# Grouped-query attention on one core: ten output staging buffers, K copies on the GpSimd queue, and a re-costed plan with groups of five

## The chip, the core and the metric

The kernel runs on one core of a Trainium2 chip. The metric is the device time of one execution in microseconds (us). Below it is the median of 13 executions; one further view comes from an execution that was profiled, whose own time is given beside its span (first to last instruction).

## What is computed

Eight batches, eight query heads, two K/V heads (each serves four query heads), 1024 positions, head dimension 64, all in float32:

```python
scores = scale * np.matmul(q_group, k_group.transpose(0, 1, 3, 2))
attn = np.exp(scores - scores_max)
attn = attn / (np.sum(attn, axis=-1, keepdims=True) + 1e-08)
output[:, q_start:q_end, :, :] = np.matmul(attn, v_group)
```

## The kernel before, in words

**Tiling.** A job is one batch, one query head and one half of its queries (the even or the odd positions, 512 of them): 8 x 8 x 2 = 128 jobs, in order. A job has eight cells, one for each 128 keys: 1024 cells. For each cell TensorE makes a score tile of 128 keys by 512 queries with one matmul (L351), an engine turns it into exponentials in bf16, and four output matmuls (L414) multiply it with V, to which a column of ones is added so that the sum of the exponentials comes out as column 65. The scores are small, so the maximum is not subtracted.

**Two ways to the exponential.** "A" cells go to ScalarE in pairs: two scores in one PSUM tile (two such tiles), one activation over 128x1024 (`exps`, L362) into a `pa` tile (26 of them). "D" cells go to VectorE: `exp_bits` (L371) turns one score from one of two PSUM banks into the bits of a bf16 in a slot of a `pd` group of four cells, and when a group is full `exp_curve` corrects it in a chain of four operations over the whole group (L386, L392, L402, L406).

**End of a job.** `normalise` takes the reciprocal of the sums (L427), multiplies the output bank with it into a staging tile `ost` (L429, four buffers, and four of `rec`), and stores that from SyncE's queue (L435). There are two output banks, and L429 is what frees one.

**Loading.** `cast` (L248, GpSimd's queue) copies a head of Q, K or V as bf16 to a scratch in DRAM; it waits for the latest score matmul in program order, so that the loads keep pace. `transpose` (L260, SyncE's queue) brings Q and K from there transposed into `qT` and `kT`, in two pieces each. `place_k` (L268, SyncE's queue) copies `kT` in four DMAs into `kset`, a form in which K stands in one half of the partitions and zeros in the other, so that one matmul with 128 rows takes only the wanted half of `qT`. `place_v` (L282, SyncE's queue) brings V in two DMAs. The very first heads are loaded by `first_loads`: K, Q and V of batch 0 in float32, cast on VectorE, ScalarE and GpSimd, and K and Q transposed on TensorE.

**What sets the order.** `make_plan` is a small planner in Python that runs while the program is built. It holds a cost for each operation and, step by step, takes the one that could start first: a score for ScalarE or VectorE, an output matmul group, a normalisation, a step of a chain. Limits keep it in bounds: `LIVE_A` and `LIVE_D` are the tiles in use, `PENDING` the cells on their way through VectorE, and the last `ONLY_A` cells go to ScalarE alone. Its times fix only the order in which instructions are written out; every engine and every queue then runs its own in that order. The loads are sorted in by their lead before a head's first score `th`: the cast of Q at th − 28, of K at th − 38 and V at th − 33, transposes of K from th − 27 and of Q from th − 17, `place_k` at th − 20, `place_v` at th − 15.

Of the kernel before, what the change touches and what calls it, by code (L numbers as in the profile page):

```python
# [11 lines left out]

CURVE_A, CURVE_B = 0.32988085, -0.33401025

GROUP = 4


def make_plan(nj, nkc):
# [3 lines left out]

    QK, PV, EXP, P1, NORM = 0.214, 0.143, 0.925, 0.605, 0.57
    CHAIN = (0.73, 0.73, 1.26, 1.26)
    FROM_PE, FROM_ACT, FROM_DVE = 0.28, 0.18, 0.12
    LIVE_A, LIVE_D, PENDING, ONLY_A = 26, 6, 8, 14
    INF = 1e9
    n = nj * nkc  # L30
    ops = []
# [14 lines left out]
    while normed < nj:  # L46
        best = None
        if nxt < n:
            ta = td = INF
            if open_a is not None:  # L50
                ta = max(pe, open_a["t"])
            elif live["A"] < LIVE_A:
                ta = max(pe, min(a_free))
            if pending < PENDING and nxt < n - ONLY_A and (cur or live["D"] < LIVE_D):
                td = max(pe, min(bank))
            t, to_d = (ta, 0) if ta <= td else (td, 1)
            if t < INF:
                best = min(best or (INF,), (t, 1 + to_d, "qk", to_d))
        for i, s in enumerate(open_jobs):
            for c in rem[s]:  # L60
                at = max(pe, ready.get(s * nkc + c, INF))
                if at < INF:
                    best = min(best or (INF,), (at, 3 + i, "pv", (s, c)))
        if len(open_jobs) < 2 and next_job < nj:
            at = max(pe, min(obank_free), min(ready.get(next_job * nkc + c, INF) for c in range(nkc)))
            if at < INF:
                best = min(best or (INF,), (at, 3 + len(open_jobs), "open", next_job))
        for q, p, kind in ((normq, 0, "norm"), (p1q, 1, "p1"), (chainq, 2, "chain")):
# [1 line left out]
                best = min(best or (INF,), (max(dve, q[0][0]), p, kind, 0))  # L70
        if cur and nxt >= n - ONLY_A and not p1q:
            best = min(best or (INF,), (dve, 9, "flush", 0))
        t, _, kind, arg = best
        if kind == "qk":
            cell = nxt
            nxt += 1
            pe = t + QK
            if not arg:
                if open_a is None:
                    slot = first_free(a_free)  # L80
                    a_id += 1
                    live["A"] += 1
                    open_a = {"slot": slot, "t": a_free[slot], "cells": []}
                    a_free[slot] = INF
                o = open_a
                ops.append((t, "qk", cell, "A", a_id, o["slot"], len(o["cells"])))
                o["cells"].append(cell)
                home[cell] = ("A", a_id)
                if len(o["cells"]) == 2 or nxt >= n:
                    act = max(act, pe + FROM_PE)  # L90
                    ops.append((act, "exp", a_id, tuple(o["cells"])))
                    act += EXP * len(o["cells"]) / 2
                    a_free[o["slot"]] = act + FROM_ACT
                    uses[("A", a_id)] = len(o["cells"])
                    for x in o["cells"]:
                        ready[x] = act + FROM_ACT
                    open_a = None
            else:
                k = first_free(bank)
                bank[k] = INF  # L100
                pending += 1
                ops.append((t, "qk", cell, "D", k, 0, 0))
                p1q.append((pe + FROM_PE, cell, k))
        elif kind == "open":
            o = first_free(obank_free)
            obank[arg] = o
            obank_free[o] = INF
            open_jobs.append(arg)
            rem[arg] = list(range(nkc))
            next_job += 1  # L110
        elif kind == "pv":
            s, c = arg
            cell = s * nkc + c
            opens = len(rem[s]) == nkc
            rem[s].remove(c)
            done = not rem[s]
            ops.append((t, "pv", s, cell, opens, done, obank[s]))
            pe = t + PV
            h = home[cell]
            uses[h] -= 1  # L120
            if not uses[h]:
                live[h[0]] -= 1
            if done:
                open_jobs.remove(s)
                normq.append((pe + FROM_PE, s))
        elif kind == "norm":
            s = normq.pop(0)[1]
            ops.append((t, "norm", s))
            dve = t + NORM
            obank_free[obank[s]] = dve + FROM_DVE  # L130
            normed += 1
        elif kind == "p1":
            _, cell, k = p1q.pop(0)
            if not cur:
                d_id += 1
                live["D"] += 1
            ops.append((t, "p1", cell, k, d_id, len(cur)))
            dve = t + P1
            bank[k] = dve + FROM_DVE
            cur.append(cell)  # L140
            home[cell] = ("D", d_id)
            if len(cur) == GROUP:
                chainq.append((dve, d_id, cur, 0))
                cur = []
        elif kind == "flush":
            chainq.append((dve, d_id, cur, 0))
            cur = []
        else:
            _, g, cells, step = chainq.pop(0)
            ops.append((t, "chain", g, len(cells), step))  # L150
            dve = t + CHAIN[step] * len(cells) / GROUP
            if step + 1 < len(CHAIN):
                chainq.insert(0, (dve, g, cells, step + 1))
            else:
                pending -= len(cells)
                uses[("D", g)] = len(cells)
                for x in cells:
                    ready[x] = dve + FROM_DVE
# [4 lines left out]
def kernel(  # L163
# [25 lines left out]
    NQS = QBS // 128  # L189
    E1 = D + 1  # L190
    PIECE = 256
    scale = 1.0 / math.sqrt(D)
    bits_scale = 128.0 * scale * math.log2(math.e)
    bits_bias = 128.0 * 127.0
# [12 lines left out]
    first_pool = ctx.enter_context(tc.tile_pool(name="firstp", bufs=1))  # L207
    qT_pool = ctx.enter_context(tc.tile_pool(name="qTpool", bufs=8))
    kT_pool = ctx.enter_context(tc.tile_pool(name="kTpool", bufs=4))
    pa_pool = ctx.enter_context(tc.tile_pool(name="papool", bufs=26))  # L210
    pd_pool = ctx.enter_context(tc.tile_pool(name="pdpool", bufs=6))
    tmp_pool = ctx.enter_context(tc.tile_pool(name="tmppool", bufs=2))
    ostage_pool = ctx.enter_context(tc.tile_pool(name="ostage", bufs=4))
    recip_pool = ctx.enter_context(tc.tile_pool(name="recip", bufs=4))

    def psum_pools(name, n):
        return [
# [21 lines left out]
    qT = {}  # L239
# [25 lines left out]
        transpose(("k", b, g), kT[(b, g)], n)  # L265

    def place_k(b, g, side, parity):
        nc.sync.dma_start(  # L268
            out=ksets[b % 2][
                side * D : (side + 1) * D, g, side, parity * HALF : (parity + 1) * HALF  # L270
            ],
# [16 lines left out]

    def first_loads():

        staged = []
        for eng, src in ((nc.sync, k[0, 0]), (nc.scalar, q[0, 0])):
            f = first_pool.tile([128, NHC, 2, D], FP32, name=f"f{len(staged)}")
            eng.dma_start(
                out=f, in_=src.rearrange("(c p two) d -> p c two d", p=128, two=2)
            )
            staged.append(f)
        vf = first_pool.tile([128, NHC, 2, D], FP32, name="vf")
        nc.sync.dma_start(
            out=vf, in_=v[0, 0].rearrange("(c p two) d -> p c two d", p=128, two=2)  # L300
        )
        cast(("q", 0, 1), q[0, 1])
        for two in range(2):
            nc.gpsimd.tensor_copy(
                out=vsets[0][:, 0, two * NHC : (two + 1) * NHC, 0:D],
                in_=vf[:, :, two, :],
            )
        for side in range(2):
            nc.gpsimd.memset(ksets[1][(1 - side) * D : (2 - side) * D, :, side, :], 0.0)  # L309
        fk, fq = staged  # L310

        hk = first_pool.tile([128, NHC, 3, D], BF16, name="hk")
        nc.vector.tensor_copy(out=hk[:, :, 0:2, :], in_=fk)  # L313
        nc.vector.tensor_copy(out=hk[:, :, 2, :], in_=fk[:, :, 0, :])
        hq = first_pool.tile([128, NHC, 2 * D], BF16, name="hq")
        nc.scalar.copy(out=hq, in_=fq.rearrange("p c two d -> p c (two d)"))
        tk = dbanks[0].tile([128, 2, HALF], BF16, name="dps0")
        tq = dbanks[1].tile([128, HALF], BF16, name="dps1")
        for w in range(2):
            for c in range(NHC):  # L320
                nc.tensor.transpose(  # L321
                    tk[:, w, c * 128 : (c + 1) * 128],
                    hk[:, c, w : w + 2, :].rearrange("p w d -> p (w d)"),
                    ident,
                )
        for c in range(NHC):
            nc.tensor.transpose(tq[:, c * 128 : (c + 1) * 128], hq[:, c, :], ident)
        qT[(0, 0)] = qT_pool.tile([128, HALF], BF16, name="qT")
        lo, hi = slice(0, D), slice(D, 2 * D)
        nc.vector.tensor_copy(out=ksets[0][lo, 0, 0, 0:HALF], in_=tk[lo, 0, :])  # L330
        nc.scalar.copy(out=qT[(0, 0)], in_=tq)
        nc.vector.tensor_copy(out=ksets[0][lo, 0, 0, HALF:S], in_=tk[lo, 1, :])
        nc.vector.tensor_copy(out=ksets[0][hi, 0, 1, 0:HALF], in_=tk[hi, 1, :])
        nc.vector.tensor_copy(out=ksets[0][hi, 0, 1, HALF:S], in_=tk[hi, 0, :])

    p_of = {}
    psum = {}
# [168 lines left out]
```

## Time and profile before

| | |
|---|---|
| median of 13 executions | 443.45 us (441.13 to 448.04) |
| profiled execution | 442.64 us, span 440.9 us |
| busy: TensorE, VectorE, ScalarE, GpSimd | 375.9, 375.8, 385.8, 55.1 us |
| mean granted clock of TensorE | 0.973 |
| exponentials on ScalarE, cells on VectorE | 412 (two cells each), 200 |
| DMA: transposes, stores, K copies, V copies, casts | 156, 128, 60, 30, 93 |

How to read the lines: PE is TensorE, PEld its weight loads, DVE VectorE, ACT ScalarE, POOL GpSimd, SP SyncE; SPq and POOLq are their DMA issues. L351 is line 351 of the kernel. "Idle before, <-" names what ended an engine's idle time just ahead of an instruction. In a line of waits stand the total in us, the number of times and the longest. In a timeline stand start, length, engine, line, operation, tiles, and how many were merged. In a table by stretch stands the busy time of each engine, then the granted clock (1.00 is full), the DMA share and GB/s. In a group the last figures are busy us, mean ns of one, and idle us before them. In a tile's view durations are minimum/median/maximum in ns.

### The profile page before, as it was taken

What the parts mean: (1) busy time and instruction counts of PE and PEld (TensorE: products, weight loads), DVE (VectorE), ACT (ScalarE), POOL (GpSimd) and SP (SyncE); (2) the same over time, 40 slices, a digit from 0 to 9 for tenths busy, and PEclk for the clock granted to TensorE, in tenths of its full rate; (3) what the DMA queues carried; (4) which work ended last, traced back from release to release, by engine and by line L of the source; (5) the groups of instructions that cost most, each with busy time, mean ns of one, the idle gap of its engine ahead of it and who ended that gap; (6) DMA issues with size and microseconds to landing.
All of it is one profiled execution on the core that took longest, in us unless ns stands there. A gap on an engine that the chain in (4) does not pass through costs nothing.

```text
span 440.9 us, 12680 instructions
## 1 busy us (share of the span) xinstructions
PE 375.9 (85%) x5043; PEld 235.7 (53%) x5132; DVE 375.8 (85%) x664; ACT 385.8 (88%) x415; POOL 55.1 (13%) x105
## 2 busy tenths in 40 slices
PE   4788799599996999789979969998959998797995
PEld 2355465355654556455655545565536655454654
DVE  5898798599996998789898959979959998698995
ACT  4899699499996999879989977998959999799993
POOL 5311101001010110101111110110101101100000
PEclk9999899789998999989999998999989999999999
DMA  3854566547576484656647565574755747555314
GB/s 95 132 97 91 116 114 112 111 90 115 108 123 116 89 134 84 121 105 110 115 95 138 111 109 97 103 130 99 121 105 91 126 91 125 110 100 113 74 38 85
DMA packets 137771, 46.73 MB, mean 106 GB/s; under 512 B 130848, under 2 KB 136224, under 8 KB 136224
## 3 DMA queue, kind: packets, MB, share of 16 engines
q1 hardware_dynamic: 134208, 33.46, 36.2%
q0 software_dynamic: 2976, 12.20, 21.3%
q8 instruction: 40, 0.66, 0.7%
q10 hardware_dynamic: 528, 0.26, 0.2%
q14 instruction: 19, 0.16, 0.1%
HBM read 27.13 MB, written 28.97 MB: 127 GB/s over the span
## 4 chain that ended last, share of the span: by engine, by line
DVE 42%; PE 19%; DMA 13%; ACT 13%; SPq 6%; issue 5%; POOL 1%; DVEq 0%; ACTq 0%
ACT pa L362 13%; DMA out_dram<-ost 10%; DVE pd L371 10%; PE aps L351 9%; DVE y L402 8%; DVE pd L406 8%; PE ops L414 8%; DVE ost L429 6%; DVE y L392 4%; SPq L260 4%; DVE z L386 3%; DVE rec L427 2%; PE dps L351 2%; DMA qT<-scr_q 1%; SPq L282 1%
## 5 line engine op out<-in xcount | busy, mean ns | idle before, releaser
L362 ACT ACTIVATE pa<-aps 128x1024 bf16<-128x1024 f32 x412 | 383.3, 1050 | 42.6 <-PE aps L351 30.1
L351 PE MATMUL aps<-qT,kset 128*128 128x512 bf16 x735 | 232.0, 388 | 14.9 <-ACT pa L362 11.5
L414 PEld LDWEIGHTS <-pa 128*128 128x128 bf16 x3296 | 138.1, 99 | 91.5 <-issue 20.3
L414 PE MATMUL ops<-vset,pa 128*128 128x65 bf16 x3296 | 149.8, 195 | 32.3 <-DVE ost L429 28.4
L371 DVE TENSOR_SCALAR pd<-dps 128x512 uint16<-128x512 f32 x200 | 129.8, 682 | 2.2 <-PE dps L351 2.1
L351 PEld LDWEIGHTS <-kset 128*128 128x128 bf16 x1024 | 84.9, 99 | 66.5 <-issue 32.0
L429 DVE TENSOR_TENSOR ost<-ops,rec 128x256 f32<-128x256 f32 x128 | 54.4, 425 | 47.4 <-DMA out_dram<-ost 43.6
L248 POOL DMA_DIRECT2D scr_q<-in_q_dram x63 | 34.7, 552 | 300.3 <-PE aps L351 259.1
L351 PE MATMUL dps<-qT,kset 128*128 128x512 bf16 x200 | 66.0, 387 | 0.9
L406 DVE TENSOR_TENSOR pd<-pd,y 128x2048 uint16<-128x2048 uint16 x50 | 61.2, 1225 | 1.7
L402 DVE TENSOR_TENSOR y<-z,y 128x2048 f16<-128x2048 uint16 x50 | 61.2, 1225 | 1.7
L414 PEld LDWEIGHTS <-pd 128*128 128x128 bf16 x800 | 38.2, 97 | 38.0 <-DVE pd L406 17.4
L414 PE MATMUL ops<-vset,pd 128*128 128x65 bf16 x800 | 45.3, 194 | 7.8 <-DVE pd L406 6.4
L392 DVE TENSOR_SCALAR y<-z 128x2048 f16<-128x2048 uint16 x50 | 34.3, 687 | 0.6
L386 DVE TENSOR_SCALAR z<-pd 128x2048 uint16<-128x2048 uint16 x50 | 34.2, 684 | 0.0
L427 DVE RECIPROCAL rec<-ops 128x4 f32<-128x4 f32 x128 | 22.4, 175 | 4.4 <-PE ops L414 3.8
L248 POOL DMA_DIRECT2D scr_k<-in_k_dram x15 | 7.7, 513 | 22.4 <-PE aps L351 16.9
L248 POOL DMA_DIRECT2D scr_v<-in_v_dram x15 | 7.5, 502 | 15.5 <-PE aps L351 14.7
L321 PE MATMUL dps<-ident,hk 128*128 128x128 bf16 x8 | 1.0, 310 | 5.1 <-DVE hk L313 5.1
L309 POOL MEMSET kset<- 64x2048 bf16 x2 | 3.6, 1798 | 0.1
L321 PEld LDWEIGHTS <-hk 128*128 128x128 bf16 x8 | 0.8, 140 | 5.1 <-DVE hk L313 5.1
L236 DVE MEMSET kset<- 64x1024 uint32 x2 | 1.8, 912 | 1.3 <-PEq L490 1.0
(19 smaller groups left out, 7.9 us busy)
## 6 DMA issues: line engine op xcount, KB each, us to landing
out_dram<-ost SPq DMA_DIRECT2D x128, 128.0 KB, 2.7
scr_q<-in_q_dram POOLq DMA_DIRECT2D x63, 128.0 KB, 3.1
kset<-kT SPq DMA_DIRECT2D x60, 64.0 KB, 2.9
qT<-scr_q SPq DMA_TRANSPOSE x126, 3.2
scr_k<-in_k_dram POOLq DMA_DIRECT2D x15, 128.0 KB, 3.3
scr_v<-in_v_dram POOLq DMA_DIRECT2D x15, 128.0 KB, 3.5
vset<-scr_v SPq DMA_DIRECT2D x30, 64.0 KB, 3.0
kT<-scr_k SPq DMA_TRANSPOSE x30, 3.5
```

Source lines behind the costliest of these rows:

```text
L248: dma = nc.gpsimd.dma_start(out=scr.rearrange("(p f) -> p f", f=1024), in_=src.rearrange("(p s) d -> p (s d)", s=1024 // D),)
L260: nc.sync.dma_start_transpose(out=dst[:, rows], in_=src[rows, :])
L351: last_score[0] = nc.tensor.matmul(dst, lhsT=ksets[b % 2][:, h // HPG, side, c * 128 : (c + 1) * 128], rhs=qT[(b, h)], start=True, stop=Tr ...
L362: nc.scalar.activation(out=pt[:, 0:m], in_=psum.pop(("A", n))[:, 0:m], func=AF.Exp, scale=scale)
L371: nc.vector.tensor_scalar(out=groups[g][:, slot], in0=psum.pop(cell), scalar1=bits_scale, scalar2=bits_bias, op0=ALU.mult, op1=ALU.add,)
L386: nc.vector.tensor_scalar(out=z, in0=pd, scalar1=0x7F, scalar2=None, op0=ALU.bitwise_and)
L392: nc.vector.tensor_scalar(out=y, in0=temps[g][0], scalar1=CURVE_A / 128.0, scalar2=CURVE_B, op0=ALU.mult, op1=ALU.add,)
L402: nc.vector.tensor_tensor(out=y, in0=z, in1=y, op=ALU.mult)
L406: nc.vector.tensor_tensor(out=pd, in0=pd, in1=y, op=ALU.add)
L414: nc.tensor.matmul(ops_of[s][:, qs, :], lhsT=p_of[cell][:, qs * 128 : (qs + 1) * 128], rhs=vsets[b % 2][:, h // HPG, c, :], start=opens an ...
L427: nc.vector.reciprocal(out=rec, in_=o[:, :, D])
L429: nc.vector.tensor_tensor(out=ost, in0=o[:, :, 0:D], in1=rec.unsqueeze(2).to_broadcast([128, NQS, D]), op=ALU.mult,)
```

## The change

Ten `ost` and ten `rec` buffers in place of four. `place_k` issues from GpSimd's queue. Groups of five cells in place of four, with 32 `pa` and five `pd` tiles. The plan has new costs, each with a fixed part and one by the cell for the exponential and the chain; a score for ScalarE may be put `AHEAD` (0.08) earlier in the order than its bank is free; no output matmuls before 2.0; the last 26 cells go to ScalarE alone. `first_loads` brings K and Q in halves, moves the cast of Q head 1 behind GpSimd's copies of V, runs 28 matmuls on the identity ahead of the first transposes, and takes the transposes and copies half by half.

```diff
-GROUP = 4
+GROUP = 5
...
-    QK, PV, EXP, P1, NORM = 0.214, 0.143, 0.925, 0.605, 0.57
-    CHAIN = (0.73, 0.73, 1.26, 1.26)
+    QK, PV, P1, NORM = 0.216, 0.122, 0.605, 0.57
+    EXP, CHAIN = (0.067, 0.4267), ((0.20, 0.133),) * 2 + ((0.19, 0.27),) * 2
     FROM_PE, FROM_ACT, FROM_DVE = 0.28, 0.18, 0.12
-    LIVE_A, LIVE_D, PENDING, ONLY_A = 26, 6, 8, 14
+    LIVE_A, LIVE_D, PENDING, ONLY_A, AHEAD, FIRST_PV = 32, 5, 7, 26, 0.08, 2.0
...
-                best = min(best or (INF,), (t, 1 + to_d, "qk", to_d))
+                early = 0.0 if to_d else AHEAD
+                best = min(best or (INF,), (t - early, 1 + to_d, "qk", to_d, t))
...
-                at = max(pe, ready.get(s * nkc + c, INF))
+                at = max(pe, FIRST_PV, ready.get(s * nkc + c, INF))
...
-            at = max(pe, min(obank_free), min(ready.get(next_job * nkc + c, INF) for c in range(nkc)))
+            at = max(pe, FIRST_PV, min(obank_free), min(ready.get(next_job * nkc + c, INF) for c in range(nkc)))
...
-        t, _, kind, arg = best
+        t, _, kind, arg = best[:4]
         if kind == "qk":
+            t = best[4]
...
-                    act += EXP * len(o["cells"]) / 2
+                    act += EXP[0] + EXP[1] * len(o["cells"])
...
-            dve = t + CHAIN[step] * len(cells) / GROUP
+            dve = t + CHAIN[step][0] + CHAIN[step][1] * len(cells)
...
+    WARM = 28
...
-    pa_pool = ctx.enter_context(tc.tile_pool(name="papool", bufs=26))
-    pd_pool = ctx.enter_context(tc.tile_pool(name="pdpool", bufs=6))
+    pa_pool = ctx.enter_context(tc.tile_pool(name="papool", bufs=32))
+    pd_pool = ctx.enter_context(tc.tile_pool(name="pdpool", bufs=5))
...
-    ostage_pool = ctx.enter_context(tc.tile_pool(name="ostage", bufs=4))
-    recip_pool = ctx.enter_context(tc.tile_pool(name="recip", bufs=4))
+    ostage_pool = ctx.enter_context(tc.tile_pool(name="ostage", bufs=10))
+    recip_pool = ctx.enter_context(tc.tile_pool(name="recip", bufs=10))
...
     def place_k(b, g, side, parity):
-        nc.sync.dma_start(
+        nc.gpsimd.dma_start(
...
+        for eng, f, src in ((nc.sync, fk, k[0, 0]), (nc.scalar, fq, q[0, 0])):
+            for half in halves:
+                eng.dma_start(
+                    out=f[:, half], in_=src.rearrange(rows, p=128, two=2)[:, half]
+                )
+        nc.sync.dma_start(out=vf, in_=v[0, 0].rearrange(rows, p=128, two=2))
-        cast(("q", 0, 1), q[0, 1])
         for two in range(2):
             nc.gpsimd.tensor_copy(
                 out=vsets[0][:, 0, two * NHC : (two + 1) * NHC, 0:D],
                 in_=vf[:, :, two, :],
             )
+        cast(("q", 0, 1), q[0, 1])
         for side in range(2):
             nc.gpsimd.memset(ksets[1][(1 - side) * D : (2 - side) * D, :, side, :], 0.0)
+
+        warm = obanks[1].tile([128, 128], FP32, name="ops1")
+        for n in range(WARM):
+            nc.tensor.matmul(warm, lhsT=ident, rhs=ident, start=True, stop=True)
...
+        for half in halves:
+            nc.vector.tensor_copy(out=hk[:, half, 0:2, :], in_=fk[:, half])
+            turn_k(0, half)
+            nc.scalar.copy(
+                out=hq[:, half], in_=fq[:, half].rearrange("p c two d -> p c (two d)")
+            )
+            for c in range(NHC)[half]:
+                nc.tensor.transpose(tq[:, c * 128 : (c + 1) * 128], hq[:, c, :], ident)
         nc.scalar.copy(out=qT[(0, 0)], in_=tq)
...
+        nc.vector.tensor_copy(out=hk[:, :, 2, :], in_=fk[:, :, 0, :])
+        put_k(0, 0, slice(0, NHC))
+        turn_k(1, slice(0, NHC))
+        put_k(0, 1, slice(0, NHC))
+        put_k(1, 0, slice(0, NHC))
+        put_k(1, 1, slice(0, NHC))
```

`turn_k` transposes a half of K with TensorE into the bank `tk`, and `put_k` copies a part of it on VectorE to its place in `kset`.

More of the change, by code (lines that the diff above doesn't have):

```diff
@@ L289, in first_loads @@
     def first_loads():
[L291 to L297, printed above, removed]
-        vf = first_pool.tile([128, NHC, 2, D], FP32, name="vf")
-        nc.sync.dma_start(
-            out=vf, in_=v[0, 0].rearrange("(c p two) d -> p c two d", p=128, two=2)
-        )
-        cast(("q", 0, 1), q[0, 1])
+        fk = first_pool.tile([128, NHC, 2, D], FP32, name="fk")
+        fq = first_pool.tile([128, NHC, 2, D], FP32, name="fq")
+        vf = first_pool.tile([128, NHC, 2, D], FP32, name="vf")
+        rows = "(c p two) d -> p c two d"
+        halves = (slice(0, NHC // 2), slice(NHC // 2, NHC))
+        for eng, f, src in ((nc.sync, fk, k[0, 0]), (nc.scalar, fq, q[0, 0])):
[4 more added lines that the diff above has]
+        nc.sync.dma_start(out=vf, in_=v[0, 0].rearrange(rows, p=128, two=2))
         for two in range(2):
@@ L307, in first_loads, with turn_k @@
             )
+        cast(("q", 0, 1), q[0, 1])
         for side in range(2):
             nc.gpsimd.memset(ksets[1][(1 - side) * D : (2 - side) * D, :, side, :], 0.0)
-        fk, fq = staged
+        warm = obanks[1].tile([128, 128], FP32, name="ops1")
+        for n in range(WARM):
+            nc.tensor.matmul(warm, lhsT=ident, rhs=ident, start=True, stop=True)
         hk = first_pool.tile([128, NHC, 3, D], BF16, name="hk")
-        nc.vector.tensor_copy(out=hk[:, :, 0:2, :], in_=fk)
-        nc.vector.tensor_copy(out=hk[:, :, 2, :], in_=fk[:, :, 0, :])
         hq = first_pool.tile([128, NHC, 2 * D], BF16, name="hq")
-        nc.scalar.copy(out=hq, in_=fq.rearrange("p c two d -> p c (two d)"))
         tk = dbanks[0].tile([128, 2, HALF], BF16, name="dps0")
         tq = dbanks[1].tile([128, HALF], BF16, name="dps1")
-        for w in range(2):
-            for c in range(NHC):
+        qT[(0, 0)] = qT_pool.tile([128, HALF], BF16, name="qT")
+        lo, hi = slice(0, D), slice(D, 2 * D)
+        def turn_k(w, half):
+            for c in range(NHC)[half]:
                 nc.tensor.transpose(
@@ L325, in first_loads, with put_k @@
                 )
[L326 to L330, printed above, removed]
-        nc.scalar.copy(out=qT[(0, 0)], in_=tq)
-        nc.vector.tensor_copy(out=ksets[0][lo, 0, 0, HALF:S], in_=tk[lo, 1, :])
-        nc.vector.tensor_copy(out=ksets[0][hi, 0, 1, 0:HALF], in_=tk[hi, 1, :])
-        nc.vector.tensor_copy(out=ksets[0][hi, 0, 1, HALF:S], in_=tk[hi, 0, :])
+        def put_k(side, parity, half):
+            part = (lo, hi)[side]
+            cols = slice(half.start * 128, half.stop * 128)
+            nc.vector.tensor_copy(
+                out=ksets[0][part, 0, side, parity * HALF : (parity + 1) * HALF][:, cols],
+                in_=tk[part, side ^ parity, cols],
+            )
[4 more added lines that the diff above has]
+                out=hq[:, half], in_=fq[:, half].rearrange("p c two d -> p c (two d)")
+            )
+            for c in range(NHC)[half]:
+                nc.tensor.transpose(tq[:, c * 128 : (c + 1) * 128], hq[:, c, :], ident)
+        nc.scalar.copy(out=qT[(0, 0)], in_=tq)
+        nc.vector.tensor_copy(out=hk[:, :, 2, :], in_=fk[:, :, 0, :])
[4 more added lines that the diff above has]
+        put_k(1, 1, slice(0, NHC))
     p_of = {}
```

## The prediction

> **What bounds the kernel now.** I read the page's first part, then the waits, then ScalarE's and VectorE's timelines, then SyncE's queue.
>
> ```profile
> span 440.9 us, 12680 instructions
> PE 375.9 (85%) x5043; PEld 235.7 (53%) x5132; DVE 375.8 (85%) x664; ACT 385.8 (88%) x415; POOL 55.1 (13%) x105
> ```
>
> Three engines stand at 85 to 88% and none at 100%, so either something stops them all at times, or they take turns. The waits tell which.
>
> ```profile
> DVE ost L429 <- DMA out_dram<-ost: 43.6, 20, 5.1
> PE ops L414 <- DVE ost L429: 28.4, 16, 4.3
> ACT pa L362 <- PE aps L351: 30.1, 26, 4.6
> ACT pa L362 <- remote: 10.8, 7, 3.9
> ```
>
> VectorE stood 20 times, 43.6 us in all, at the write into an output staging buffer, because the store that last used this buffer had not landed. TensorE then waited for VectorE (28.4 us), since the output bank that it needs next is freed by that same instruction, and ScalarE waited for TensorE. One instance, from the two timelines:
>
> ```profile
> 84.75 0.42 DVE L429 TENSOR_TENSOR ost<-ops,rec 128x256 f32<-128x256 f32 x1 [4.60 <-DMA out_dram<-ost]
> 86.78 1.02 ACT L362 ACTIVATE pa<-aps 128x1024 bf16<-128x1024 f32 x1 [4.44 <-PE aps L351]
> ```
>
> VectorE's 4.60 us come back as 4.44 us of ScalarE two microseconds later. Between such events ScalarE has no gap, and the table by stretch shows what a free stretch looks like beside one with stalls.
>
> ```profile
> core 0: us, PE busy (x) PEld busy (x) DVE busy (x) ACT busy (x) POOL busy (x), PEclk, DMA share, GB/s
> 40.00:90.00 50.00, 41.16 (x510) 24.86 (x520) 39.96 (x68) 40.15 (x43) 5.43 (x11) 0.90 0.61 111
> 142.00:176.00 34.00, 32.18 (x455) 20.64 (x461) 31.50 (x57) 34.00 (x38) 4.07 (x8) 1.00 0.58 102
> ```
>
> With stalls ScalarE is busy 40.15 of 50 us and the granted clock is 0.90; free of them 34.00 of 34 and 1.00. So a kernel without the stalls is set by ScalarE's 412 exponentials, with VectorE close behind (31.50 of 34).
>
> Why the stores are late is in SyncE's queue, which issues in order:
>
> ```profile
> 71.92 3.41 SPq L268 DMA_DIRECT2D kset<-kT  x4
> 76.72 3.40 SPq L260 DMA_TRANSPOSE qT<-scr_q  x2
> 80.21 1.08 SPq L282 DMA_DIRECT2D vset<-scr_v  x2
> 81.39 1.01 SPq L435 DMA_DIRECT2D out_dram<-ost  x2
> ```
>
> The two stores of 81.39 went out behind 3.41 us of K copies, 3.40 of transposes and 1.08 of V copies; the wait that ended at 84.75 is for one of them.
>
> **The change, part by part.** ScalarE's own account of the present span is the frame of the sum:
>
> ```profile
> L362 ACT ACTIVATE pa<-aps 128x1024 bf16<-128x1024 f32 x412 | 383.3, 1050 | 42.6 <-PE aps L351 30.1
> 8.28 10.27 ACT L362 ACTIVATE pa<-aps 128x1024 bf16<-128x1024 f32 x11 [1.10 <-PE aps L351]
> 20.48 20.28 ACT L362 ACTIVATE pa<-aps 128x1024 bf16<-128x1024 f32 x22 [1.92 <-PE aps L351]
> 406.45 26.69 ACT L362 ACTIVATE pa<-aps 128x1024 bf16<-128x1024 f32 x29 [0.55 <-PE aps L351]
> ```
>
> First exponential at 8.28; 383.3 busy; 42.6 − 1.10 = 41.5 idle after the first; last one ends at 406.45 + 26.69 = 433.14, which leaves 440.9 − 433.14 = 7.8 of tail. 8.28 + 383.3 + 41.5 + 7.8 = 440.9. The profiled execution took 442.64, 1.7 more than its span, and the median of the 13 runs is 443.45, 0.8 above that.
>
> *Staging buffers, 4 to 10.* 128 stores in 441 us are one per 3.4 us, so four buffers cover about 14 us from one use to the next and ten cover 34 us. The queue rows above put about 9 us of other issues ahead of a pair of stores; ten buffers hold that three times over. I take the whole 43.6 us of VectorE's wait as gone, and with it 41.5 − 1.92 = 39.6 us of ScalarE's idle time (the 1.92 at 20.48 is a start-up matter, below). What is late next is ScalarE itself. Small gaps will stay: I put 2 us, between 0 (the free stretch has none) and 10 (a quarter of what goes).
>
> *K copies to GpSimd.* Sixty issues leave SyncE and join GpSimd.
>
> ```profile
> L268 SPq DMA_DIRECT2D kset<-kT x60: 472/596/1547, 21.3 to 392.9; - x60
> L260 SPq DMA_TRANSPOSE qT<-scr_q x126: 1102/1234/3077, 6.2 to 411.2; - x126
> L260 SPq DMA_TRANSPOSE kT<-scr_k x30: 1115/1234/2383, 15.5 to 385.1; - x30
> L435 SPq DMA_DIRECT2D out_dram<-ost x128: 372/532/1967, 31.7 to 437.6; - x128
> L282 SPq DMA_DIRECT2D vset<-scr_v x30: 452/534/1762, 28.5 to 400.0; - x30
> L248 POOL DMA_DIRECT2D scr_q<-in_q_dram x63: 486/486/1003, 1.3 to 397.1; - x63
> ```
>
> By medians SyncE issues 60 x 0.596 + 156 x 1.234 + 128 x 0.532 + 30 x 0.534 = 312 us now and 277 after, 69% of a 400 us span. It stays below its limit, so I count this as nothing on the path; it makes the first edit safer. On GpSimd the nearest row is the cast: 0.486 to 1.003 us an issue, so 60 copies take 29 to 60 us of an engine that is 13% busy. In order, four copies wait there for both K transposes to land, and behind them stand the paced casts of later Q heads. The copies' room:
>
> ```profile
> 391.00 3.32 SPq L268 DMA_DIRECT2D kset<-kT  x4
> 0.00:406.00 406.00, 257.48 (x875) 79.56 (x958) 0.97 0.61 109
> ```
>
> By 406.00, 958 score weights had been loaded, so the group that these copies feed (cell 960) is first read just after 406: 15 us behind the start of the copies, the last K group of the run. The copies with their landing take 3.3 + 2.9 (the page's median for kset), leaving about 9 us. The cost is taken at zero; cover gone, it is a rival below.
>
> A rule speaks against this part. The Trainium skill, page "SBUF — State Buffer", section "SBUF: two separate sides", says that a DMA issued from GpSimd cannot get its descriptors written while VectorE runs an operation in a two-port mode, and the page has a 620 ns DMA become 3100 ns so. By that page's figures, as an estimate, four copies would be some 10 us later, a microsecond more than there is room, and the sum 15 us more, 416. This trace does not bear it out for the casts, which run beside a VectorE that is 85% busy at a median equal to their minimum, 0.486 us.
>
> *Groups of five.*
>
> ```profile
> L402 DVE TENSOR_TENSOR y<-z,y 128x2048 f16<-128x2048 uint16 x50 | 61.2, 1225 | 1.7
> L406 DVE TENSOR_TENSOR pd<-pd,y 128x2048 uint16<-128x2048 uint16 x50 | 61.2, 1225 | 1.7
> L392 DVE TENSOR_SCALAR y<-z 128x2048 f16<-128x2048 uint16 x50 | 34.3, 687 | 0.6
> L386 DVE TENSOR_SCALAR z<-pd 128x2048 uint16<-128x2048 uint16 x50 | 34.2, 684 | 0.0
> ```
>
> A chain costs 2 x 1.225 + 0.687 + 0.684 = 3.82 us for four cells. The work grows with the cells and only a fixed part per instruction is saved; bounds are 0 and all that a chain costs beyond its elements. The plan's new constants (0.20 and 0.19 fixed) lie between, and as an estimate 0.17 x 4 instructions x 10 chains fewer = 6.8 us less VectorE, with VectorE not the bound. It is worth something only if the plan gives VectorE more cells. Its costs per cell fall by 0.5% for ScalarE (0.925 to 0.920 a pair) and by 2% for VectorE (0.605 + 3.98/4 = 1.600 to 0.605 + 4.81/5 = 1.567), so the split stays near today's 200 cells; ending VectorE's share 12 cells earlier takes back some 2. I take 413 exponentials, from 408 to 420. The last 29 of the row above took 26.69/29 = 0.920 each: 413 x 0.921 = 380.4.
>
> *A score that waits for its bank.* The plan lets a ScalarE score go up to 0.08 us ahead of its bank's release; queued behind it on TensorE are output matmuls. At most 413 x 0.08 = 33 us.
>
> ```profile
> 9.36 0.59 PE L351 MATMUL aps<-qT,kset 128*128 128x512 bf16 x2
> 434.23 2.63 PE L414 MATMUL ops<-vset,pa 128*128 128x65 bf16 x80
> ```
>
> A pair of scores adds 0.59 − 0.38 = 0.21 a matmul, the output matmuls 2.63/80 = 0.033: 1024 x 0.21 + 4096 x 0.033 = 350 us of a 400 us span. The 50 us left cover the 33, so I cost it at nothing.
>
> *Start.* K and Q come in halves, 28 matmuls run before the transposes, and the cast of Q head 1 moves behind the V copies.
>
> ```profile
> 1.33 0.62 POOL L248 DMA_DIRECT2D scr_q<-in_q_dram  x1 [0.21 <-issue]
> 5.84 0.74 POOL L304 CAST vset<-vf 128x256 bf16<-128x256 f32 x2 [3.50 <-DMA vf<-in_v_dram]
> 6.64 3.65 POOL L309 MEMSET kset<- 64x2048 bf16 x2
> 14.21 5.50 DMA qT<-scr_q
> ```
>
> The first exponential may come 1.2 us earlier (four scores that took 0.42 each instead of 0.21, and halves). Against it, the cast goes from 1.33 to about 6.6; with 3.1 to land and two transposes (1.23 more, 3.2 to land) head 1 is ready at about 14, and its first score ran at 12.25: some 2 us of stall. Head 2's Q, which stopped TensorE until 19.85, still hangs on GpSimd's 3.65 us of clearing and lands near 19.7. So all gains and losses end at the same gate, and I leave 8.28 + 1.92 = 10.2 as it is, from 9 to 13.
>
> *Tail.* Eighty output matmuls, 2.63 us, were still queued at 434.23. VectorE's last chain now ends 12 cells earlier; I take 6.5 of 7.8, from 5 to 8.
>
> Sum: 10.2 + 380.4 + 2 + 6.5 = 399.1 of span, 400.8 with the 1.7, and 401.5 as a median (0.7 above).
>
> **The rivals.** (1) VectorE's saving counts in full: 440.9 − 43.6 − 6.8 = 390.5 of span, 393 as a median, if the plan moves cells to VectorE until both end together. For it: VectorE has no other idle time; against: ScalarE's 0.92 x 412 alone leaves no room. (2) Part of the gain goes to a new wait: each two-operand operation over five cells holds VectorE 0.3 us longer (1.225/4), so a score for VectorE waits for its bank with ScalarE's next score behind it. Two such operations are 0.6 us a chain; if 0.4 of it reaches ScalarE, forty chains make 16 us: 417. For it are the 0.5 us gaps after stalls; against, the free stretch. (3) SyncE's issue rate is the true limit and ten buffers only move the wait: then 60 copies off the queue are matched by other waits and the time stays within 0.3%. Against: 71% by medians. (4) Slower: GpSimd becomes the gate of each K group, its issues held up beside VectorE or waiting for transposes. (The Trainium skill's "SBUF — State Buffer", named above, states such a hold.) It decides once the copies come more than the 9 us late; to pass 444.8, (444.8 − 401.5)/15 = 2.9 us must be lost at each of 15 K groups, so copies 12 us late. Eleven more microseconds in four issues is 2.7 each beyond what SyncE took; the casts' worst is 0.5 above their median. At that point the time would be 446.
>
> **How the numbers follow.** Forecast (396 to 407) 0.67; rival 1 (389 to 396) 0.13; rival 2 (407 to 425) 0.145; rival 3 0.015; rival 4 0.04. Below 394 I leave about 0.07, above 412 about 0.07 of rival 2 and the 0.055 of the last two: range 394 to 412. About 0.3% is what a measurement of this kernel can tell from no change. Faster 0.945, same 0.015, slower 0.04.
>
> **What would show it.** Right: the wait of ost for its store under 3 us in all; ScalarE above 94% of the span with gaps only before 20 us; kset issues on GpSimd's queue; VectorE with 39 to 41 chains of 128x2560; clock above 0.99. Rival 2 shows as ScalarE waiting for scores with the chain's operations as releasers, rival 4 as score weights waiting for kset copies. An ost wait above 20 us, or ScalarE idle over 25 us, would make the prediction wrong.

## The result, and the profile after

The changed kernel takes 399.91 us (median of 11 executions, 398.92 to 401.28) against 444.05 (48 executions of the kernel before): ratio 0.905, 95% interval 0.9026 to 0.9075. The forecast was 401.5, in a range of 394 to 412. Ratios here and below are formed from undisturbed executions alone, medians from all. The number was right, and the part of the change that the prediction credited with it was not, as the experiments show.

The head of the page after, its costliest group on ScalarE, and ScalarE's timeline from its first exponential to its last:

```profile
span 398.1 us, 12676 instructions
PE 366.5 (92%) x5072; PEld 233.4 (59%) x5160; DVE 368.8 (93%) x621; ACT 384.3 (97%) x418; POOL 89.4 (22%) x165
L383 ACT ACTIVATE pa<-aps 128x1024 bf16<-128x1024 f32 x414 | 381.6, 1064 | 5.8 <-PE aps L372 4.3
```

```profile
6.70 2.86 ACT L383 ACTIVATE pa<-aps 128x1024 bf16<-128x1024 f32 x3 [0.68 <-PE aps L372]
9.94 1.94 ACT L383 ACTIVATE pa<-aps 128x1024 bf16<-128x1024 f32 x2 [0.39 <-PE dps L372]
14.80 1.94 ACT L383 ACTIVATE pa<-aps 128x1024 bf16<-128x1024 f32 x2 [2.92 <-PE aps L372]
16.94 3.88 ACT L383 ACTIVATE pa<-aps 128x1024 bf16<-128x1024 f32 x4 [0.21 <-PE aps L372]
21.32 29.70 ACT L383 ACTIVATE pa<-aps 128x1024 bf16<-128x1024 f32 x32 [0.49 <-PE aps L372]
51.25 342.18 ACT L383 ACTIVATE pa<-aps 128x1024 bf16<-128x1024 f32 x371 [0.23 <-ACT pa L383]
```

From 21 us on ScalarE runs without a gap that matters: 371 exponentials in one stretch of 342 us. The wait of `ost` for a store has gone from the list of waits. The four longest waits that remain are GpSimd's own, and one of them is new. It stands here with the K copies' durations on that queue (minimum/median/maximum in ns):

```profile
POOL kset L271 <- DMA kT<-scr_k: 69.3, 14, 8.4
```

```profile
L271 POOL DMA_DIRECT2D kset<-kT x60: 518/527/916, 22.3 to 352.6; - x60
```

GpSimd stands in front of the K copies until K's transposes land, 69.3 us in 14 times, and no engine waits for it. An issue takes a median of 0.527 us (0.518 to 0.916) beside a VectorE that is 93% busy.

### The profile page after: what moved, and what is told of

Read it like the earlier page. It is cut to its first block, busy times and chain, and to the rows that moved or that the text cites. A ratio compares the mean times of both kernels' runs of the same rounds, so it can differ in the third digit from the quotient of the medians.

```text
span 398.1 us, 12676 instructions
## 1 busy us (share of the span) xinstructions
PE 366.5 (92%) x5072; PEld 233.4 (59%) x5160; DVE 368.8 (93%) x621; ACT 384.3 (97%) x418; POOL 89.4 (22%) x165
## 4 chain that ended last, share of the span: by engine, by line
ACT 71%; PE 13%; issue 5%; DVE 5%; DMA 3%; POOL 1%; SPq 1%
ACT pa L383 71%; PE aps L372 6%; PE ops L435 6%; DVE pd L392 2%; DMA qT<-scr_q 2%; PE dps L372 1%; DMA vf<-in_v_dram 1%; POOL kset L312 1%; DVE ost L450 1%; DMA scr_q<-in_q_dram 1%; DVE y L413 1%; DVE z L407 1%; DVE y L423 0%; DVE pd L427 0%; DVE rec L448 0%
## 5 line engine op out<-in xcount | busy, mean ns | idle before, releaser
L383 ACT ACTIVATE pa<-aps 128x1024 bf16<-128x1024 f32 x414 | 381.6, 1064 | 5.8 <-PE aps L372 4.3
L372 PE MATMUL aps<-qT,kset 128*128 128x512 bf16 x740 | 228.0, 380 | 19.0 <-ACT pa L383 15.6
L423 DVE TENSOR_TENSOR y<-z,y 128x2560 f16<-128x2560 uint16 (+1 forms) x40 | 58.5, 1464 | 1.1
L427 DVE TENSOR_TENSOR pd<-pd,y 128x2560 uint16<-128x2560 uint16 (+1 forms) x40 | 58.5, 1463 | 1.0
L435 PEld LDWEIGHTS <-pd 128*128 128x128 bf16 x784 | 40.7, 97 | 24.1 <-DVE pd L427 1.9
L271 POOL DMA_DIRECT2D kset<-kT x60 | 33.1, 562 | 80.4 <-DMA kT<-scr_k 69.3
L435 PE MATMUL ops<-vset,pd 128*128 128x65 bf16 x784 | 49.3, 193 | 0.5
L407 DVE TENSOR_SCALAR z<-pd 128x2560 uint16<-128x2560 uint16 (+1 forms) x40 | 32.3, 809 | 0.7
L413 DVE TENSOR_SCALAR y<-z 128x2560 f16<-128x2560 uint16 (+1 forms) x40 | 32.3, 807 | 0.2
L316 PE MATMUL ops<-ident 128*128 128x128 bf16 x28 | 3.2, 313 | 1.4 <-POOL ident masks.py:199 1.4
L316 PEld LDWEIGHTS <-ident 128*128 128x128 bf16 x28 | 2.9, 149 | 1.4 <-POOL ident masks.py:199 1.4
```

Source lines behind the costliest of these rows:

```text
L271: nc.gpsimd.dma_start(out=ksets[b % 2][side * D : (side + 1) * D, g, side, parity * HALF : (parity + 1) * HALF], in_=kT[(b, g)][parity * D ...
L372: last_score[0] = nc.tensor.matmul(dst, lhsT=ksets[b % 2][:, h // HPG, side, c * 128 : (c + 1) * 128], rhs=qT[(b, h)], start=True, stop=Tr ...
L383: nc.scalar.activation(out=pt[:, 0:m], in_=psum.pop(("A", n))[:, 0:m], func=AF.Exp, scale=scale)
L407: nc.vector.tensor_scalar(out=z, in0=pd, scalar1=0x7F, scalar2=None, op0=ALU.bitwise_and)
L413: nc.vector.tensor_scalar(out=y, in0=temps[g][0], scalar1=CURVE_A / 128.0, scalar2=CURVE_B, op0=ALU.mult, op1=ALU.add,)
L423: nc.vector.tensor_tensor(out=y, in0=z, in1=y, op=ALU.mult)
```

## The experiments

Three theories were set up after the result. The first is the prediction's: the **ten buffers** take VectorE's wait away. The second: **SyncE's queue** was the limit, and the 60 K copies taken off it are the gain. The third: the **new plan** is. Each run is timed against the kernel before on its own chip, whose median lay between 445 and 447 us in these comparisons, so ratios compare better than microseconds.

### Ten buffers alone

```diff
-    ostage_pool = ctx.enter_context(tc.tile_pool(name="ostage", bufs=4))
-    recip_pool = ctx.enter_context(tc.tile_pool(name="recip", bufs=4))
+    ostage_pool = ctx.enter_context(tc.tile_pool(name="ostage", bufs=10))
+    recip_pool = ctx.enter_context(tc.tile_pool(name="recip", bufs=10))
```

> The kernel before with one edit: ten ost and ten rec buffers; K copies stay on SyncE, plan and start as before. Theory 1 (the buffers do it): VectorE's 43.6 us of waiting for the stores go; start 10.2, 412 exponentials of 0.921, 2 us of gaps, tail 7.8, so about 402 us (400 to 406), ost wait under 3 us. Theory 2 (SyncE's queue is the limit, and taking the K copies off it is what does it): the lag only grows into the larger reserve, time above 425 us, ost or qT waits above 25 us. Theory 3 (the new plan does it): above 425 us.

Measured: 438.68 us, ratio 0.978 (0.968 to 0.987). Its waits, and below them TensorE's wait for Q in the kernel before:

```profile
ACT pa L362 <- PE aps L351: 39.0, 34, 3.2
PE aps L351 <- DMA qT<-scr_q: 30.3, 22, 3.0
PEld L351 <- DMA qT<-scr_q: 8.8, 6, 3.1
```

```profile
PE aps L351 <- DMA qT<-scr_q: 2.1, 1, 2.1
```

The wait of `ost` is gone, as the prediction said. In its place TensorE waits for Q's transposes: 30.3 us at the matmuls and 8.8 at their weight loads. ScalarE loses 39.0 us to TensorE, against 30.1 and 10.8 before. A queue that falls behind delays whatever it carries. With four buffers the stores ran out first; with ten the lag grows until the next deadline, Q's, is missed. The traces show the lag: between the landing of a head's Q and the first weight load for its scores lay 7.2 us before (median of 63 heads), and 1.2 us here, with 30 heads under 0.5.

### K copies on GpSimd alone

```diff
     def place_k(b, g, side, parity):
-        nc.sync.dma_start(
+        nc.gpsimd.dma_start(
```

> The kernel before with one edit: the 60 K copies issue from GpSimd; four buffers remain. Theory 1: stores still stand behind transposes and V copies with four buffers; the stalls at K bursts shrink but 15 to 30 us of ost wait remain, 418 to 432 us. Theory 2: SyncE is relieved of some 3 us at each of 15 K groups, the wait is nearly gone, 400 to 408 us. Theory 3: within 5 us of before.

Measured: 402.81 us, ratio 0.900 (0.892 to 0.907): nearly the whole gain from one word. (The profiled execution, from which the views are, took 399.33.) With four buffers and the old plan, the wait for stores and ScalarE's last stretch are:

```profile
DVE ost L429 <- DMA out_dram<-ost: 2.4, 2, 2.0
```

```profile
51.05 338.75 ACT L362 ACTIVATE pa<-aps 128x1024 bf16<-128x1024 f32 x368 [0.37 <-PE aps L351]
```

Four buffers were enough as soon as the queue kept up: 2.4 us of the 43.6 are left.

### The changed kernel with four buffers

```diff
-    ostage_pool = ctx.enter_context(tc.tile_pool(name="ostage", bufs=10))
-    recip_pool = ctx.enter_context(tc.tile_pool(name="recip", bufs=10))
+    ostage_pool = ctx.enter_context(tc.tile_pool(name="ostage", bufs=4))
+    recip_pool = ctx.enter_context(tc.tile_pool(name="recip", bufs=4))
```

> The changed kernel with four ost and four rec buffers again, everything else kept. Theory 1: the ost wait is back with 15 to 30 us, 415 to 430 us. Theory 2: the K copies are off SyncE, so it stays at 400 to 405 us. Theory 3: 400 to 405 us.

Measured: 400.25 us, ratio 0.896 (0.889 to 0.902), the changed kernel's time. The six buffers more are worth nothing that can be measured here.

### The changed kernel with the K copies on SyncE

```diff
     def place_k(b, g, side, parity):
-        nc.gpsimd.dma_start(
+        nc.sync.dma_start(
```

> The changed kernel with the K copies on SyncE again, ten buffers kept. Theory 1: the buffers cover it, 399 to 402 us, ost wait under 3 us. Theory 2: SyncE's lag grows until transposes of Q come late or the ten buffers run out, above 415 us. Theory 3: 399 to 402 us.

Measured: 442.72 us, ratio 0.985 (0.974 to 0.996). All else in the change stays, and the gain is gone. Again it is Q that comes late:

```profile
PE aps L372 <- DMA qT<-scr_q: 33.5, 27, 3.1
PEld L372 <- DMA qT<-scr_q: 21.3, 16, 3.2
```

The first and third theories fall with these four runs. Two readings of the second remained. Either SyncE's time is what counts (S), or the K copies as such do the harm, by what they wait for or who waits for them (K).

### V copies off the queue instead

The kernel before with ten buffers; K copies stay on SyncE.

```diff
     def place_v(b, g):
         for two in range(2):
-            nc.sync.dma_start(
+            nc.gpsimd.dma_start(
```

> The kernel before with ten buffers; K copies stay on SyncE and the 30 V copies go to GpSimd instead. Theory S: SyncE loses the some 22 us that the V bursts take in its timeline, out of a queue that sets the pace with 437 us, so 410 to 420 us. Theory K (the K copies as such do the harm, by what they wait for or who waits for them): 432 to 440 us, as with ten buffers alone.

Measured: 417.65 us, ratio 0.935 (0.930 to 0.940), against 438.68 with the ten buffers alone. The V copies have nothing to do with K, and taking them off gives back about what they took: 21.0 us of time (19 by the ratios) for the 20.8 us that the V copies' issues sum to in the run with the ten buffers alone. The wait of TensorE's score matmuls for Q falls from 30.3 to 13.0 us:

```profile
PE aps L351 <- DMA qT<-scr_q: 13.0, 10, 3.0
```

### Spare copies put on the queue

The changed kernel, with a second copy of K issued from SyncE at each place, into tiles that nobody reads. It does more work than the computation needs.

```diff
             in_=kT[(b, g)][parity * D : (parity + 1) * D, :],
         )
+        spare = spare_pool.tile([128, HALF], BF16, name="spare")
+        nc.sync.dma_start(
+            out=spare[side * D : (side + 1) * D, :],
+            in_=kT[(b, g)][parity * D : (parity + 1) * D, :],
+        )
```

> The changed kernel with 60 more copies of K on SyncE, of the same shape and at the same places, into spare tiles that nobody reads; the real copies stay on GpSimd. Theory S: SyncE gets back some 49 us of work and the time goes to 432 to 445 us, with TensorE waiting for Q's transposes. Theory K: nobody waits for the spare copies, 399 to 404 us.

Measured: 421.90 us, ratio 0.938 (0.932 to 0.944); the profiled execution took 418.88. Nobody waits for the spare copies and the kernel is slower, with TensorE waiting for Q:

```profile
L279 SPq DMA_DIRECT2D spare<-kT x60: 472/592/1414, 23.4 to 378.6; - x60
```

```profile
PE aps L378 <- DMA qT<-scr_q: 12.9, 9, 2.5
PEld L378 <- DMA scr_q<-in_q_dram: 13.4, 10, 2.4
PE dps L378 <- DMA qT<-scr_q: 4.7, 2, 3.3
```

The spare copies stand behind the same transposes as the real ones did, but SyncE did not stop for that: its list of waits has no row for them, nor for the K copies in the kernel before. So K is out, and S stands in kind. Its size does not: 432 to 445 was expected, because I put the K copies at 49 us. The spare ones took 37.5 us of issues, and the transposes beside them were 23 us shorter in sum than in the changed kernel (218.0 for 241.3). An issue's time seems to be partly elastic; more on that below.

### Transposes in one piece

The kernel before with ten buffers; K and V copies stay on SyncE, and each head's transpose is one DMA of 512 rows, not two of 256.

```diff
-    PIECE = 256
+    PIECE = 512
```

> The kernel before with ten buffers and transposes of 512 rows in place of two of 256: 78 issues of SyncE fewer, the same bytes; K and V copies stay on SyncE. If a transpose's time on SyncE is by the issue, the queue loses 78 of some 1.2 to 1.5 us, about 100 us, is no bound any more and the time is 400 to 406 us, ScalarE's. If it is by the rows moved, nothing is saved and it stays at 432 to 440 us as with ten buffers alone.

Measured: 398.07 us, ratio 0.890 (0.886 to 0.895). The lowest ratio of all, though the intervals of others reach into it, with the old plan and the old start and without one DMA moved to another queue. It is below the 400 to 406 that was expected. The first row below is from the run with ten buffers alone, the second from this one:

```profile
L260 SPq DMA_TRANSPOSE qT<-scr_q x126: 1103/1232/3690, 6.3 to 412.9; - x126
```

```profile
L260 SPq DMA_TRANSPOSE qT<-scr_q x63: 1122/1200/4101, 6.0 to 364.5; - x63
```

```profile
19.56 369.20 ACT L362 ACTIVATE pa<-aps 128x1024 bf16<-128x1024 f32 x401 [0.18 <-PE aps L351]
```

Twice the rows, the same 1.2 us: here a transpose costs SyncE by the issue. The sums say the same, 188.4 us for the 126 and 97.9 for the 63. With half as many the queue has room, ScalarE does 401 of its 412 exponentials in one stretch, and TensorE's waits for Q's transposes come to 1.1 us. The run also answers a rival that the others leave, the load on the DMA engines themselves: the bytes are the same (46.73 MB with the ten buffers alone, 46.71 here).

### The old plan in the changed kernel

The planner of before with groups of four, 26 `pa` and six `pd` tiles; all else as changed.

```diff
-GROUP = 5
+GROUP = 4
...
-    LIVE_A, LIVE_D, PENDING, ONLY_A, AHEAD, FIRST_PV = 32, 5, 7, 26, 0.08, 2.0
+    LIVE_A, LIVE_D, PENDING, ONLY_A = 26, 6, 8, 14
```

> The changed kernel with the planner of before (its costs and limits, groups of four, 26 pa and 6 pd tiles); buffers, K copies on GpSimd and the new start kept. Theory S (SyncE's queue is what bounded the kernel before, the K copies off it are the whole gain): the plan is worth only its tail and VectorE's fixed parts, 400 to 404 us. Theory P (the new plan makes a part of the gain): above 408 us.

Measured: 401.11 us, ratio 0.900 (0.896 to 0.903). The new plan is worth some 1 us at most, less than these runs can tell from nothing.

### Four runs on the start

The cast of Q head 1 ahead of the V copies again:

```diff
+        cast(("q", 0, 1), q[0, 1])
         for two in range(2):
             nc.gpsimd.tensor_copy(
...
-        cast(("q", 0, 1), q[0, 1])
```

> The changed kernel with the cast of Q head 1 ahead of GpSimd's copies of V again, all else kept. If the 2.7 us in which TensorE waits for that head's Q at 14 us counts in full, 397 us; if the next head's Q is a gate of its own close behind, as the prediction had it, or if the early cast slows the first loads by as much, 399 to 401 us.

Measured: 398.05 us, ratio 0.893 (0.891 to 0.896), between the two expectations.

GpSimd clears the second `kset` first, then casts, then copies V:

```diff
+        for side in range(2):
+            nc.gpsimd.memset(ksets[1][(1 - side) * D : (2 - side) * D, :, side, :], 0.0)
+        cast(("q", 0, 1), q[0, 1])
         for two in range(2):
             nc.gpsimd.tensor_copy(
...
-        cast(("q", 0, 1), q[0, 1])
-        for side in range(2):
-            nc.gpsimd.memset(ksets[1][(1 - side) * D : (2 - side) * D, :, side, :], 0.0)
```

> The changed kernel with GpSimd's start in another order: the two clearings of 3.65 us first, then the cast of Q head 1, then the copies of V. The cast goes at about 5.0 in place of 6.3 and the next casts at about 6.4 in place of 10.6; the first loads are not disturbed. TensorE's stall for head 1 shrinks from 2.7 to about 1.4 us: 398.0 to 398.8 us; if only the sum of both gates counts as the prediction had it, 399.5 to 400.5.

Measured: 399.53 us, ratio 0.894 (0.890 to 0.897).

The cast between the two clearings:

```diff
+        nc.gpsimd.memset(ksets[1][D : 2 * D, :, 0, :], 0.0)
+        cast(("q", 0, 1), q[0, 1])
+        nc.gpsimd.memset(ksets[1][0:D, :, 1, :], 0.0)
         for two in range(2):
             nc.gpsimd.tensor_copy(
```

> As the run before it, with the cast of Q head 1 between the two clearings, at about 3.2 us, when the first halves of K and Q are in. If it slows the second halves less than a cast at 1.3 did (which put the first exponential from 6.7 to 7.8), no stall is left and the time is 396.5 to 397.5 us; if as much, 398 us like that run.

Measured: 399.52 us, ratio 0.893 (0.890 to 0.897), above both expectations. And the changed kernel beside these two on their chip:

> The changed kernel once more, for comparison on the same chip as the three runs beside it: 399 to 401 us by every theory.

Measured: 400.99 us, ratio 0.897 (0.892 to 0.901). TensorE's warm-up matmuls and ScalarE's first exponential show where the two clearing runs lost what they won; first the changed kernel's warm-up row (its exponential stands above), then the run that clears first, then the early cast:

```profile
1.41 3.17 PE L316 MATMUL ops<-ident 128*128 128x128 bf16 x28 [1.41 <-POOL ident masks.py:199]
```

```profile
1.19 1.80 POOL L306 MEMSET kset<- 64x2048 bf16 x1
3.07 0.29 POOL masks.py:199 TENSOR_SCALAR_AFFINE_SELECT ident<-ident 128x128 bf16<-128x128 bf16 x1
3.42 3.17 PE L316 MATMUL ops<-ident 128*128 128x128 bf16 x28 [3.42 <-POOL ident masks.py:199]
8.74 2.85 ACT L383 ACTIVATE pa<-aps 128x1024 bf16<-128x1024 f32 x3 [0.68 <-PE aps L372]
14.30 0.38 PE L372 MATMUL dps<-qT,kset 128*128 128x512 bf16 x1 [0.95 <-DMA qT<-scr_q]
```

```profile
2.40 3.17 PE L316 MATMUL ops<-ident 128*128 128x128 bf16 x28 [2.40 <-POOL ident masks.py:199]
7.80 2.85 ACT L383 ACTIVATE pa<-aps 128x1024 bf16<-128x1024 f32 x3 [0.68 <-PE aps L372]
```

In the run that clears first the stall for head 1 fell from 2.7 to 0.95 us, more than expected (1.4), and still the time did not come to 398.0 to 398.8. A clearing (1.19) came in front of GpSimd's last step on the identity matrix (3.07), so the warm-up, and the transposes queued behind it, began 2.0 us later and the first exponential came at 8.74 and not 6.70. The early cast has the same fault by half (2.40, 7.80; ScalarE's cast of Q's second half, too, started at 5.65 there and at 4.65 in the changed kernel) and comes out 2 us under the changed kernel's 399.91; the two were not timed on the same chip, so that is no settled gain. By their intervals the two clearing runs are not to be told from the changed kernel beside them.

## Why the prediction was right, and where it was wrong

The table adds up the durations of SyncE's single issues in each run's trace, with the profiled execution's span beside it. (A row of a timeline that merges several issues holds the spaces between them too.)

| run | issues on SyncE, us | span, us | difference |
|---|---|---|---|
| before | 377.6 | 440.9 | 63 |
| ten buffers alone | 380.9 | 437.0 | 56 |
| changed, K on SyncE | 385.7 | 442.2 | 57 |
| ten buffers, V on GpSimd | 360.1 | 416.2 | 56 |
| changed, spare copies | 361.8 | 417.1 | 55 |
| changed | 340.8 | 398.1 | 57 |
| K on GpSimd alone | 335.4 | 397.5 | 62 |
| transposes whole | 267.3 | 396.2 | 129 |

**What bounded the kernel.** The prediction's first step, VectorE stops at a late store and ScalarE gets the gap back, is right. The next was wrong: it asked how long a buffer must last and not whether the queue keeps up. In the four slow versions below the first row the span is the issues plus 55 to 57 us: about 4 before the first issue and after the last, 9 of waiting for the first two casts, 12 to 14 near the end, when only stores are left to issue, and the rest some 0.085 us ahead of each issue. Between, for 380 us and more, no space is longer than 0.51 us, and in the kernel before none is longer than 0.44 up to 408 us. That is a full queue. With whole transposes 67 us of longer spaces lie in that stretch.

**The step that failed** is "By medians SyncE issues ... 312 us now ... I count this as nothing on the path". The median of a transpose is 1.234 us, but 156 of them took 232.2 us, 1.49 each; K copies took 0.79 each for a median of 0.596, stores 0.59 for 0.532. With the V copies it is 378 and not 312, and after the change 341 and not 277; the spaces between issues, left out altogether, come on top with some 30 us. A queue's load is a sum, and a median of a skewed duration hides it. The same step's other half, "ten buffers hold that three times over", took a lag for a burst: the buffers measured 1 to 3% by themselves, the K copies 9 to 11%. Rival 3 had the right limit, "SyncE's issue rate is the true limit and ten buffers only move the wait", and the wrong outcome: it let the moved copies be made up by other waits, so that it stood for no change at 0.015.

The Trainium skill, page "Perfetto Trace Analysis", section "What "DMA-bound" means", lists this case: a kernel can be bound by the issuing engine's sequencer, whose track is then solid with DMA slices. SyncE's timeline before agrees, with no space over 0.44 us from 13 to 408 us, and so do the runs.

**Why the number held.** Whatever took the stalls away, ScalarE was next, and its account needs no cause. That the number held was luck as to the cause: the part that the prediction counted on gives 438.68 by itself, and one that it counted at nothing, which happened to be in the same change, gives 402.81. Term by term, forecast and measured: start and its stall 10.2 against 6.70 + 4.24 = 10.9 (the five gaps in brackets above, 0.39 to 0.23); exponentials 380.4 against 381.6, with 414 of them for 413; small gaps 2 against 0.9; tail 6.5 against 398.1 − 393.4 = 4.7. The sum is 399.1 against 398.1. The start went as the working had it: the first exponential 1.6 us earlier, and a stall of 2.7 us for head 1, "some 2 us"; head 2's Q landed at 20.9 and not near 19.7.

**The other parts.** GpSimd's issues cost nothing on the path, as forecast: no row of the list of waits has TensorE behind a K copy. Their durations above, with a median of 0.527 us close to the minimum of 0.518, and their landing 2.8 us after the issue (median; 2.9 from SyncE before) do not bear out here the rule of the Trainium skill's "SBUF — State Buffer" that the prediction weighed; the profile does not tell which of VectorE's operations run in the two-port mode that the rule names. Groups of five are 40 chains, one of them short; their groups on the page after:

```profile
L423 DVE TENSOR_TENSOR y<-z,y 128x2560 f16<-128x2560 uint16 (+1 forms) x40 | 58.5, 1464 | 1.1
L427 DVE TENSOR_TENSOR pd<-pd,y 128x2560 uint16<-128x2560 uint16 (+1 forms) x40 | 58.5, 1463 | 1.0
L407 DVE TENSOR_SCALAR z<-pd 128x2560 uint16<-128x2560 uint16 (+1 forms) x40 | 32.3, 809 | 0.7
L413 DVE TENSOR_SCALAR y<-z 128x2560 f16<-128x2560 uint16 (+1 forms) x40 | 32.3, 807 | 0.2
```

They sum to 181.6 us for 196 cells, against 190.9 for 200 before, which is 187.1 for 196: 5.5 us saved for 6.8 forecast, and nothing of it on the path. Rival 1, with more cells for VectorE, did not come (196 cells), nor rival 2: no gap of ScalarE over 0.25 us after 22 us. The early score for ScalarE was not undone by itself; it leaves no cost that shows in the 0.9 us of small gaps.

**What stays open.** The changed kernel's queue is as dense as the full ones, with the same 57 us of difference and no space over 0.51 us from 13.5 to 372.9 us, yet it is not late. From the fourth head that is loaded on, Q landed 3.7 to 11.6 us ahead of the first weight load for its scores, about as much late as early (medians by thirds 7.5, 6.9 and 6.7 us; over all heads 6.8, against 12.7 with whole transposes). So part of what is counted as issue time is probably waiting that shrinks when the queue is pressed, as with the transposes beside the spare copies. What it waits for was not found. A semaphore alone it is not: K copies in the kernel before that wait for none took up to 1.46 us. How much more the changed kernel's queue would carry is known only from above: the spare copies, 37.5 us, were too much. The new start was not undone by itself either.

## What to carry to other kernels

When transfers come late, add up what their queue issues, with the spaces between, and compare it with the span, before giving the waiting engine more buffers: buffers bridge a burst, and behind a full queue they only choose which wait comes next. Fewer and larger issues can be worth as much as moving them: one constant, beside ten buffers, gave here what moving sixty copies gave. And a forecast that comes out right proves only its last term, the next bound; undo each part alone before crediting it.

## What the runs showed of the hardware

A DMA transpose's time on SyncE's queue was nearly the same for 256 and for 512 rows (median 1.232 and 1.200 us). Between two issues in a dense stretch of that queue lay some 0.085 us. The sixty K copies took a median of 0.527 us each on GpSimd (mean 0.562) and of 0.596 on SyncE (mean 0.79). TensorE's mean granted clock was 0.973 in the kernel before and 0.995 after, where TensorE has no long idle time after the start.
